# Two layers in a fast bilinear scheme: the first block's loads, casts and product order, and the order and additions of the last block

## The chip, the cores and the metric

The kernel runs on one core of a Trainium2 chip. A core has a matrix engine (TensorE, PE in the profile; its weight loads are the row PEld), VectorE (DVE), ScalarE (ACT), GpSimd (POOL) and SyncE (SP), which issues transfers only; ACT and POOL issue transfers as well, each on queues of its own. The metric is the device time of one execution in microseconds. Before the change the median of three runs is 852.05 us (851.43 to 852.44).

## The reference

```python
# x [16,512,768], w1 [768,3072], b1 [3072], w2 [3072,768], all float32, normal draws
y = np.matmul(x, w1) + b1
y = np.maximum(y, 0)
return np.matmul(y, w2).astype(np.float32)
```

The 16 x 512 rows of x are one matrix of 8192 rows. So two products of 8192 x 768 x 3072 and 8192 x 3072 x 768 are computed, with a bias and a ReLU between.

## The kernel before

**Scheme.** Both layers use a bilinear scheme with fewer products than the plain one: sums and differences of blocks of x and of w1 (and of y and of w2) are formed on VectorE, multiplied on TensorE in float16, and combined again by VectorE and ACT. Tables at the top of the file hold which sums are formed (`X_SUMS`, `W1_SUMS`, `Y_SUMS`, `W2_SUMS`), which products are taken, and in which order (`FIRST_ORDER`, `SECOND_ORDER`, and `LAST_ORDER` for the last block).

**Blocks.** There are 16 iterations: two halves (chunks) of the 3072 hidden columns, and in each the eight blocks of 1024 rows. An iteration computes the hidden layer of its block (per group of hidden columns, gi = 0 and 1, 20 products in place of 24, each of six matmuls of 128 x 256, L1071) and then eight outputs (26 products in place of 32, each of six matmuls of 128 x 384, L1197). Output number `to` is 256 rows by 384 columns. The sums of x are at L826, of w1 at L842, of w2 at L860, of y at L1044.

**First block (iteration 0).** Its first layer is computed plainly, since no sums exist yet (`first_block`, `add_plain`, products at L981). The prologue issues the loads: four tiles of 128 rows of x as float32 into the slots `s` (L711; tiles 0 and 2 on SP's queue, 1 and 3 on ACT's), the bias as 24 rows of 128 on ACT's queue behind them (L679), then on POOL's queue, which casts to float16 on the way, three strips of w1 of group 0 (each 768 rows by two lots of 128 columns in `v1`, L685), the lower 512 rows of x as float16 into `xn` (L706), the strips of group 1, and w2 (L691). x of the first block is turned on TensorE: three 128 x 128 transposes fill a bank (L923), VectorE copies one half of the columns of a tile to `x` (L931) and ACT the other (L929). The upper four tiles are turned in float32, the lower four in float16. `add_bias` turns the bias rows on TensorE (L943), copies them to `b1y` (L946), squares them (L949) and fills the tables of bias combinations (L957, L961), all of the latter on VectorE. In `first_block` it is added between the first and the second half of the first bank. Each bank takes 12 matmuls of 256 columns, six per 256 rows of x, and is then evicted by ACT with bias and ReLU into `y`. Later blocks get x turned by the DMA queue of SP (L758).

**Order.** A planner (`Graph`) receives the tasks with costs, and keys that they read and write. TensorE runs its tasks in the order in which they were added; the tasks of the other engines are put in order by a simulation with these costs, in which `presets` gives the times at which the first loads are taken to land (bias rows at 5.0, x tiles at 5.3 and 7.2, w1 strips from 9.3 on). The result is a fixed order of instructions for each engine with semaphores between them. PSUM has eight banks; `Reg` stands for one or two of them, or for one of nine slots of `s`.

**Second chunk and last block.** The outputs of the first chunk are stored plainly. Those of the second are added to them: by default by an accumulating transfer, issued by POOL (L1250; L1253 stores the part of an output apart from its last product). In the last iteration the operations in `LAST_DIRECT` go another way: `add_priors` reads the stored output back by SP into the space of x (L1172), `prior_task` adds the kept sum to it on VectorE (L1258), `operation` adds the product's bank (L1214), and SP stores the result plainly (L1248). The last output goes in two halves, stored on ACT's and on SP's queue (L1243). An operation that is also in `LAST_FOLD` has the stored output added into its bank on VectorE ahead of the chain's last product (`fold`), and is then copied out by ACT (L1208). Before the change `LAST_FOLD` names operations 6 and 7, neither of which is in `LAST_DIRECT`, so no fold takes place. `SECOND_OPS` gives the outputs: operation 5 makes output 1, operation 0 output 2, operation 1 output 3, operation 2 output 4, operations 6 and 7 outputs 6 and 7.

At the end a flag, computed from sums of squares of all inputs, decides whether a general path runs; with these inputs it doesn't.

Of the kernel before, what the change touches and what calls it, by code (L numbers as in the profile page):

```python
# [10 lines left out]
FP16 = mybir.dt.float16  # L11
# [3 lines left out]
ACTF = mybir.ActivationFunctionType  # L15
# [3 lines left out]
P = 128  # L19
# [567 lines left out]
class Fast:  # L587
# [93 lines left out]
    def load_strip(self, to, c, g, h):  # L681
# [26 lines left out]
    def prologue(self):  # L708
        nc = self.nc
        for s in range(4):  # L710
            (nc.sync, nc.scalar)[s % 2].dma_start(out=self.s[:, s],  # L711
                                                  in_=self.xf[s * P:(s + 1) * P, :])
        self.load_bias()
        self.load_strip(self.v1, 0, 0, 0)
        self.constants()
        self.load_strip(self.v1, 0, 0, 1)
        self.load_strip(self.v1, 0, 0, 2)
        self.load_x(0, 1, 2)
        for h in range(3):
            self.load_strip(self.v1, 0, 1, h)  # L720
        for q in range(4):
            for h in range(3):
                self.load_w2(self.v2, 0, h, q)
        self.load_x(1, 0)
        for _ in range(8):
            nc.tensor.matmul(self.ps[:, 7, 0:P], lhsT=self.ones, rhs=self.ones, start=True,
                             stop=True)

    def presets(self):
        g = self.g  # L730
        for t, at in enumerate((9.3, 11.3, 13.3, 19.9, 21.8, 23.8)):
            for k in range(2):
                g.preset(("w1", t // 3, 2 * (t % 3) + k), at)
# [171 lines left out]

    def add_transpose_first(self, half, s):

        for a in range(2):  # L910
            ps = Reg("ps", leaves=0)

            def view(ps=ps):
                p = self.ps[:, ps.at[0], :]
                if half:
                    p = p[:, 0:3 * P // 2].bitcast(FP16)
                return p[:, 0:3 * P].rearrange("p (k m) -> p k m", k=3)

            def turn(a=a, view=view):
                ident = (self.ident, self.ident16)[half]  # L920
                rows = self.xn[:, 4 + s, :] if half else self.s[:, s]
                for k in range(3):
                    self.nc.tensor.transpose(view()[:, k, :],  # L923
                                             rows[:, (3 * a + k) * P:(3 * a + k + 1) * P], ident)

            def copy(a=a, view=view):
                out = self.x_part(4 * half + s)[:, 3 * a:3 * a + 3]
                if a:
                    self.nc.scalar.copy(out=out, in_=view())  # L929
                else:  # L930
                    self.nc.vector.tensor_copy(out=out, in_=view())  # L931
            r = 2 * half + s // 2
            self.g.add("PE", 210 if half else 380, turn, writes=[ps],
                       reads=[("xn", 4 + s)] if half else [("rows", s), self.hold[s]])
            self.g.add("ACT" if a else "DVE", 560, copy, reads=[ps],
                       writes=[("x", 2 * r + a, s % 2)])

    def add_bias(self):
        nc = self.nc
# [29 lines left out]
    def add_plain(self, strip, j, m, parts, evict_parts, between=None):  # L969
        gi, h = divmod(strip, 3)  # L970
        ps = Reg("ps", leaves=2 if parts == 1 else 0)
        nc = self.nc
# [13 lines left out]
        def evict(a, b):  # L986
            n = 4 * h + 2 * gi + j
            i = 8 * m + 2 * gi + j
            out = self.y[:, i:i + 5:4, h * self.QM:(h + 1) * self.QM]
            nc.scalar.activation(out=out[:, a:b],  # L990
                                 in_=self.ps[:, ps.at[0], :].rearrange("p (a m) -> p a m",
                                                                       a=2)[:, a:b],
                                 func=ACTF.Relu, bias=self.b1y[:, n:n + 1])
        for n in range(parts):
            rows = (0, 1) if parts == 1 else (n,)
            nc = self.nc
            self.g.add("PE", 1300 // parts, lambda n=n: product(n),
                       reads=[("x", 4 * m + 2 * r + k2, q) for r in rows for k2 in range(2)
                              for q in range(2)] + [("w1", gi, 2 * h + k) for k in range(2)],
                       writes=[ps])  # L1000
            if n == 0 and between:
                between()
        for a, b in ((0, 2),) if evict_parts == 1 else ((0, 1), (1, 2)):
            self.g.add("ACT", 692 if evict_parts == 1 else 470, lambda a=a, b=b: evict(a, b),
                       reads=[ps, "b1y"],
                       writes=[("y", (2 * m + r) * 4 + 2 * gi + j, h) for r in range(a, b)])

    def first_block(self):
# [534 lines left out]
```

## Time and profile before

| what | value |
|---|---|
| median of three runs | 852.05 us |
| profiled execution, whole | 851.03 us |
| its span | 849.4 us |
| TensorE matmuls busy | 839.5 us, 99% |
| TensorE weight loads busy | 625.1 us, 74% |
| VectorE busy | 736.5 us, 87% |
| ACT busy | 568.5 us, 67% |
| POOL busy | 166.5 us, 20% |
| mean granted TensorE clock | 0.999 |
| moved by DMA | 128.93 MB in 170968 packets |

The profile is one execution, taken by the hardware profiler. Its span runs from the first to the last instruction on record, the execution's own time has some more around it. In the rows of the timeline, the first two numbers are the start in us from the span's start and the duration; then engine, line, operation, tiles (written <- read), shapes and the count of instructions in the stretch. In square brackets stands the idle time ahead of it and what ended it. ACTq and SPq are the issue of a transfer by that engine. A row of the view that tells who waits for whom has engine, tile and line of the waiting instruction, the one waited for, and then the sum in us, the count and the longest wait. A row of windows begins with the stretch and its length; then come, for PE, PEld, DVE, ACT, POOL and SP in this order, the busy time (and the count of instructions), the granted clock, the DMA share and the GB/s. A row of DMA queues has packets, MB and the time of its packets as a share of 16 engines; a row of landing times the count, the KB of one and the median us from issue to landing.

### The profile page before, as it was taken

Reading aid. Unit: us, or ns where it says so; the run is one execution under the profiler, and the core shown is the slowest. Engines: PE = TensorE matmul, PEld = TensorE weight load, DVE = VectorE, ACT = ScalarE, POOL = GpSimd, SP = SyncE. Lnnn points to the kernel's source line nnn. Section 1 sums busy time; section 2 is a strip of 40 time slices with the busy share of each in tenths; the row PEclk is TensorE's granted clock in tenths of the full one; section 3 lists DMA queues with packets and bytes.
Section 4 is the critical chain, followed back from the end, with each engine's and each line's share of the span. In section 5 each row is a group of like instructions: output and inputs, shape, how many; then the busy total and the mean of one; then the engine's idle time right before and its main releaser. Section 6 shows DMA issues by size and latency. Waiting matters only on the chain.

```text
span 849.4 us, 16770 instructions
## 1 busy us (share of the span) xinstructions
PE 839.5 (99%) x6381; PEld 625.1 (74%) x6381; DVE 736.5 (87%) x1229; ACT 568.5 (67%) x1203; POOL 166.5 (20%) x181
## 2 busy tenths in 40 slices
PE   8999999999999999999999999999999999999997
PEld 7558778587786867768687686877868677686874
DVE  5898988969889697988999989698896979979787
ACT  5866967678686784946859477766657666456462
POOL 5210011102111020110031503224041230502301
PEclk9999999999999999999999999999999999999999
DMA  9996597969789496593894968979789797975937
GB/s 212 202 180 175 82 230 108 198 140 160 198 109 203 117 154 164 96 249 123 232 177 82 193 109 148 160 110 176 124 130 147 122 164 113 154 126 75 167 85 178
DMA packets 170968, 128.93 MB, mean 152 GB/s; under 512 B 93805, under 2 KB 169349, under 8 KB 170885
## 3 DMA queue, kind: packets, MB, share of 16 engines
q0 software_dynamic: 57104, 69.61, 53.3%
q1 hardware_dynamic: 113312, 57.23, 28.4%
q8 instruction: 50, 0.82, 0.4%
q10 hardware_dynamic: 468, 1.00, 0.3%
q14 instruction: 34, 0.27, 0.1%
HBM read 73.15 MB, written 69.60 MB: 168 GB/s over the span
## 4 chain that ended last, share of the span: by engine, by line


## 5 line engine op out<-in xcount | busy, mean ns | idle before, releaser
L1197 PE MATMUL ps<-v,y 128*128 128x384 f16 x2496 | 408.5, 326 | 0.5 <-ACT s L1208 0.5
L1071 PE MATMUL ps<-x,v 128*128 128x256 f16 x3600 | 395.6, 273 | 0.0
L1071 PEld LDWEIGHTS <-v 128*128 128x128 f16 x3600 | 352.0, 98 | 42.5
L1197 PEld LDWEIGHTS <-y 128*128 128x128 f16 x2496 | 244.0, 98 | 160.9 <-issue 1.0
L1208 ACT ACTIVATE s<-ps 128x384 f32<-128x384 f32 (+1 forms) x244 | 153.8, 643 | 137.4 <-PE ps L1197 136.3
L1044 DVE TENSOR_TENSOR y<-y 128x768 f16<-128x768 f16 (+1 forms) x384 | 219.0, 618 | 2.5
L1114 DVE CUSTOM_DVE_ANT_0 y<-ps,s 128x512 f16<-128x512 f32 x240 | 155.7, 685 | 54.2 <-ACT s L1111 41.9
L1250 POOL DMA_DIRECT2D out_dram<-s x79 | 95.2, 1467 | 166.7 <-ACT s L1208 112.7
L1111 ACT ACTIVATE s<-ps,bt 128x256 f32<-128x256 f32 x180 | 75.1, 469 | 63.2 <-PE ps L1071 57.4
L826 DVE TENSOR_TENSOR x<-x 128x768 f16<-128x768 f16 (+1 forms) x210 | 113.8, 578 | 1.4
L706 POOL DMA_DIRECT2D xn<-in_x_dram x30 | 25.1, 838 | 258.4 <-ACT xn L766 153.8
L1111 ACT ACTIVATE y<-ps,bt 128x256 f16<-128x256 f32 x180 | 69.6, 486 | 7.7 <-PE ps L1071 7.7
L1214 DVE TENSOR_TENSOR s<-ps,s 128x768 f32<-128x768 f32 x74 | 70.5, 952 | 1.7 <-PE ps L1197 0.9
L1208 ACT ACTIVATE ps<-ps 128x384 f32<-128x384 f32 (+1 forms) x144 | 68.1, 512 | 5.0 <-PE ps L1197 3.2
L1214 DVE TENSOR_TENSOR s<-s,ps 128x768 f32<-128x768 f32 x60 | 57.0, 950 | 2.8 <-PE ps L1197 0.5
L766 ACT ACTIVATE xn<-xn 128x768 f16<-128x768 f16 x64 | 53.5, 837 | 1.2 <-DMA x<-xn 1.2
L1253 POOL DMA_DIRECT2D out_dram<-s x16 | 18.9, 1184 | 108.6 <-ACT s L1208 97.3
L1111 ACT ACTIVATE ps<-ps,bt 128x256 f32<-128x256 f32 x60 | 26.7, 445 | 19.2 <-PE ps L1071 18.2
L1107 ACT ACTIVATE ps<-ps 128x512 f32<-128x512 f32 x60 | 35.3, 588 | 3.6 <-DVE y L1114 3.5
L1122 DVE TENSOR_TENSOR s<-s,ps 128x512 f32<-128x512 f32 x30 | 20.6, 687 | 17.8 <-PE ps L1071 17.8
L981 PE MATMUL ps<-x,v 128*128 128x256 f16 (+1 forms) x216 | 32.0, 308 | 0.7 <-DVE x L931 0.7
L1117 DVE SCALAR_TENSOR_TENSOR s<-ps,bt,s 128x256 f32<-128x256 f32 x60 | 26.1, 476 | 4.4 <-PE ps L1071 4.4
(59 smaller groups left out, 302.6 us busy)
## 6 DMA issues: line engine op xcount, KB each, us to landing
out_dram<-s POOLq DMA_DIRECT2D x95, 384.0 KB, 7.6
out_dram<-s SPq DMA_DIRECT2D x69, 384.0 KB, 4.6
xn<-in_x_dram POOLq DMA_DIRECT2D x28, 768.0 KB, 9.2
v<-in_w_dram POOLq DMA_DIRECT2D x6, 384.0 KB, 10.6
v<-in_w_dram POOLq DMA_DIRECT2D x12, 192.0 KB, 9.0
w1d<-in_w_dram POOLq DMA_DIRECT2D x6, 384.0 KB, 6.8
w2d<-in_w_dram POOLq DMA_DIRECT2D x12, 192.0 KB, 5.4
v<-w1d SPq DMA_DIRECT2D x12, 192.0 KB, 4.2
```

The source lines that it names most:

```text
L766: self.nc.scalar.activation(out=self.xn[:, s, :], in_=self.xn[:, s, :], func=ACTF.Square, accum_out=self.stat[:, self.stat_at["x"] + i:][: ...
L826: self.nc.vector.tensor_tensor(out=self.two(x, out), in0=self.two(x, in0), in1=self.two(x, in1), op=ALU.add if sign > 0 else ALU.subtract)
L981: nc.tensor.matmul(self.ps[:, ps.at[0], cols], lhsT=self.v1[:, gi, 2 * h + k2, k, j * P:(j + 1) * P], rhs=rhs, start=(k2 == 0 and k == 0), ...
L1044: self.nc.vector.tensor_tensor(out=self.two(self.y, out), in0=self.two(self.y, in0), in1=self.two(self.y, in1), op=ALU.add if sign > 0 els ...
L1071: nc.tensor.matmul(self.ps[:, at, j * self.QM:(j + 1) * self.QM], lhsT=self.v1[:, gi, self.w1s[c][gi][FIRST_V[p]], k, j * P:(j + 1) * P], ...
L1107: nc.scalar.activation(out=out, in_=ps, scale=float(a), func=func if kind == "out" else ACTF.Copy)
L1111: nc.scalar.activation(out=out[:, j], in_=ps[:, j], func=func, scale=float(a), bias=beta(j))
L1114: nc.vector._custom_dve(TENSOR_ADD_SAT, out=out, in0=ps, in1=s, s0=F_MAX, s1=0.0)
L1197: nc.tensor.matmul(self.ps[:, bank[ch].at[j], 0:NH], lhsT=self.y[:, ys[SECOND_U[p]], m0:m0 + P], rhs=self.v2[:, slot[SECOND_V[p]], h, :], ...
L1208: nc.scalar.activation(out=out, in_=ps, func=ACTF.Copy, scale=float(a))
L1214: engine.tensor_tensor(out=out, in0=in0, in1=in1, op=ALU.add if a == b else ALU.subtract)
L1250: nc.gpsimd.dma_start(out=rows, in_=out, accum_op=ALU.add)
```

## The change

There are two parts.

**First block.** The three column strips of w1 of group 0 become six row pieces (`load_part`: 128 rows by three lots of 256 columns, 0.197 MB as written). The upper four tiles of x are cast from float32 to float16 into slots 16 to 19 of `y` (`add_casts`, one half of the columns on VectorE, one on ACT) and then turned in float16, six transposes to a bank in place of three. The bias is added first of all. The 72 matmuls of six banks (three strips, two column lots each) no longer run bank by bank: `first_rows` holds six banks at once and runs with the row piece k outermost, so that each piece of w1 is used by six products for one or two row halves n before the next is needed; the six evictions come after all of them. The transposes of tiles 2 and 3 stand behind the first six products, those of the lower tiles behind the steps (4, 1) and (5, 1). `presets` gets landing times for the pieces.

**Last block.** `LAST_DIRECT` takes in operation 7: output 7 is read back, added on the chip and stored plainly. `LAST_FOLD` becomes operation 5. The last thirteen products of `LAST_ORDER` stand in another order.

```diff
-LAST_ORDER = (13, 15, 4, 17, 10, 8, 12, 18, 3, 0, 1, 14, 2, 19, 23, 21, 11, 16, 25, 22, 7, 9, 6,
-    24, 5, 20)
-LAST_FOLD = (6, 7)
-LAST_DIRECT = (0, 1, 2, 3, 4, 5)
+LAST_ORDER = (13, 15, 4, 17, 10, 8, 12, 18, 3, 0, 1, 14, 2, 19, 21, 11, 25, 23, 7, 16, 5, 6, 22,
+    9, 24, 20)
+LAST_FOLD = (5,)
+LAST_DIRECT = (0, 1, 2, 3, 4, 5, 7)
...
+    def load_part(self, g, k):
+        w1r = self.w1.rearrange("(k p) (h c) -> p k h c", p=P, c=4 * P)
+        self.nc.gpsimd.dma_start(out=self.v1[:, g, k // 3:6:2, k % 3, :],
+                                 in_=w1r[:, k, 0:3, 2 * g * P:2 * (g + 1) * P])
...
         self.load_bias()
-        self.load_strip(self.v1, 0, 0, 0)
+        self.load_part(0, 0)
         self.constants()
-        self.load_strip(self.v1, 0, 0, 1)
-        self.load_strip(self.v1, 0, 0, 2)
+        for k in range(1, 6):
+            self.load_part(0, k)
         self.load_x(0, 1, 2)
...
-        for t, at in enumerate((9.3, 11.3, 13.3, 19.9, 21.8, 23.8)):
+        parts = (8.2, 9.2, 10.2, 11.2, 12.3, 13.4)
+        for k in range(6):
+            g.preset(("part", k), parts[k])
...
+    def add_casts(self):
+        for s in range(4):
+            for a in range(2):
+                cols = slice(3 * a * P, 3 * (a + 1) * P)
+                def cast(s=s, cols=cols, a=a):
+                    out, rows = self.y[:, 16 + s, cols], self.s[:, s, cols]
+                    if a:
+                        self.nc.scalar.copy(out=out, in_=rows)
+                    else:
+                        self.nc.vector.tensor_copy(out=out, in_=rows)
+                self.g.add("ACT" if a else "DVE", 560 if a else 500, cast,
+                           reads=[("rows", s), self.hold[s]], writes=[("cast", s, a)], due=0.0)
+
+    def add_transpose_first(self, half, rows):
+        for s in rows:
             ps = Reg("ps", leaves=0)
...
+            def turn(s=s, view=view):
+                tile = self.xn[:, 4 + s, :] if half else self.y[:, 16 + s, :]
+                for k in range(6):
+                    self.nc.tensor.transpose(view(k // 3)[:, k % 3, :],
+                                             tile[:, k * P:(k + 1) * P], self.ident16)
...
+    def first_rows(self):
+        nc = self.nc
+        banks = {(h, j): Reg("ps", leaves=0) for h in range(3) for j in range(2)}
+        def product(k, n, h, j):
+            nc.tensor.matmul(self.ps[:, banks[h, j].at[0], n * self.QM:(n + 1) * self.QM],
+                             lhsT=self.v1[:, 0, 2 * h + k // 3, k % 3, j * P:(j + 1) * P],
+                             rhs=self.x[:, 2 * n + k // 3, k % 3, :],
+                             start=(n == 0 and k == 0), stop=(k == 5), skip_group_check=True)
+        for k, n in ((0, 0), (1, 0), (0, 1), (1, 1), *((k, n) for k in range(2, 6) for n in range(2))):
+            for h, j in banks:
+                self.g.add("PE", 109, lambda k=k, n=n, h=h, j=j: product(k, n, h, j),
+                           reads=[("x", 2 * n + k // 3, q) for q in range(2)] + [("part", k)],
+                           writes=[banks[h, j]])
+            if (k, n) == (0, 0):
+                self.add_transpose_first(0, (2, 3))
+            elif (k, n) == (4, 1):
+                self.add_transpose_first(1, (0, 1))
+        self.add_transpose_first(1, (2, 3))
+        for h, j in banks:
+            self.add_evict(h, j, 0, banks[h, j], 1)
...
     def first_block(self):
-        for s in range(4):
-            self.add_transpose_first(0, s)
         plain = self.add_plain
-        for strip in range(3):
-            for j in range(2):
-                between = None
-                if strip == 0 and j == 0:
-                    between = self.add_bias
-                elif strip == 2 and j == 1:
-                    between = lambda: [self.add_transpose_first(1, s) for s in (0, 1)]
-                plain(strip, j, 0, 2, 2 if strip == 1 else 1, between)
-        plain(0, 0, 1, 2, 1, lambda: [self.add_transpose_first(1, s) for s in (2, 3)])
-        plain(0, 1, 1, 2, 1)
+        self.add_casts()
+        self.add_bias()
+        self.add_transpose_first(0, (0, 1))
+        self.first_rows()
+        for j in range(2):
+            plain(0, j, 1, 2, 1)
```

More of the change, by code (lines that the diff above doesn't have):

```diff
@@ L927, in copy @@
                 out = self.x_part(4 * half + s)[:, 3 * a:3 * a + 3]
                 if a:
-                    self.nc.scalar.copy(out=out, in_=view())
+                    self.nc.scalar.copy(out=out, in_=view(a))
                 else:
-                    self.nc.vector.tensor_copy(out=out, in_=view())
+                    self.nc.vector.tensor_copy(out=out, in_=view(a))
             r = 2 * half + s // 2
-            self.g.add("PE", 210 if half else 380, turn, writes=[ps],
-                       reads=[("xn", 4 + s)] if half else [("rows", s), self.hold[s]])
@@ L935, in add_transpose_first @@
-            self.g.add("ACT" if a else "DVE", 560, copy, reads=[ps],
-                       writes=[("x", 2 * r + a, s % 2)])
+            self.g.add("PE", 420, turn, writes=[ps],
+                       reads=[("xn", 4 + s)] if half else [("cast", s, a) for a in range(2)])
+            for a in range(2):
+                self.g.add("ACT" if a else "DVE", 480, lambda a=a, copy=copy: copy(a), reads=[ps],
+                           writes=[("x", 2 * r + a, s % 2)])
     def add_bias(self):
@@ L984, in product @@
                                      stop=(k2 == 1 and k == 2))
[L986 to L993, printed above, removed]
         for n in range(parts):
@@ L1002, in add_plain, with add_evict, evict @@
                 between()
+        self.add_evict(strip, j, m, ps, evict_parts)
+    def add_evict(self, strip, j, m, ps, evict_parts):
+        gi, h = divmod(strip, 3)
+        nc = self.nc
+        def evict(a, b):
+            n = 4 * h + 2 * gi + j
+            i = 8 * m + 2 * gi + j
+            out = self.y[:, i:i + 5:4, h * self.QM:(h + 1) * self.QM]
+            nc.scalar.activation(out=out[:, a:b],
+                                 in_=self.ps[:, ps.at[0], :].rearrange("p (a m) -> p a m",
+                                                                       a=2)[:, a:b],
+                                 func=ACTF.Relu, bias=self.b1y[:, n:n + 1])
         for a, b in ((0, 2),) if evict_parts == 1 else ((0, 1), (1, 2)):
```

23 lines of the change are left out of this document (8 added, 15 removed).

## The prediction

> **What bounds the kernel now.** I read the page first, then who waits for whom on TensorE, then the timeline of both ends.
>
> ```profile
> span 849.4 us, 16770 instructions
> ```
> ```profile
> PE ps L923 <- DMA s<-in_x_dram: 1.1, 2, 0.6
> PE ps L981 <- DVE x L931: 0.7, 2, 0.4
> PE ps L1197 <- ACT s L1208: 0.5, 1, 0.5
> ```
> Between its first product and its last, TensorE waits twice in all: 0.35 us for an x copy in the first block (the longer of the two L981 waits) and 0.5 us once for ACT. So everything in between is TensorE's own work, the change leaves that work as it is, and only two stretches can pay: the way to the first products, and what follows the last one. The change touches both. First the start, from the timeline:
>
> ```profile
> 1.51 0.99 POOL L685 DMA_DIRECT2D v<-in_w_dram  x1 [0.83 <-POOLq L1527]
> 1.87 0.65 ACTq L679 DMA_DIRECT2D b_rows<-in_b_dram  x1
> ...
> 6.96 2.50 POOL L685 DMA_DIRECT2D v<-in_w_dram  x3
> ...
> 7.68 1.50 PE L923 MATMUL ps<-ident,s 128*128 128x128 f32 x12 [0.52 <-DMA s<-in_x_dram]
> 8.23 1.21 DVE L931 CAST x<-ps 128x384 f16<-128x384 f32 x2 [0.81 <-PE ps L923]
> ...
> 9.50 0.82 PE L981 MATMUL ps<-x,v 128*128 128x256 f16 x6 [0.32 <-DVE x L931]
> ...
> 10.24 0.24 PE L943 MATMUL ps<-ident,b_rows 24*128 24x24 f32 x1
> ...
> 10.41 6.72 PE L981 MATMUL ps<-x,v 128*128 128x256 f16 x60
> 10.52 0.18 DVE L946 COPY b1y<-ps 128x24 f32<-128x24 f32 x1 [1.07 <-PE ps L943]
> ...
> 12.15 0.18 DVE L949 TENSOR_TENSOR stat<-b1y 128x24 f32<-128x24 f32 x1
> ...
> 16.97 0.83 PE L923 MATMUL ps<-ident,xn 128*128 128x128 f16 x12
> ...
> 17.49 0.61 DVE L931 COPY x<-ps 128x384 f16<-128x384 f16 x2
> 17.51 0.86 ACT L929 COPY x<-ps 128x384 f16<-128x384 f16 x2 [0.30 <-PE ps L923]
> ...
> 17.64 1.59 PE L981 MATMUL ps<-x,v 128*128 128x256 f16 x12
> ...
> 20.26 12.11 PE L981 MATMUL ps<-x,v 128*128 128x256 f16 x88 [0.35 <-DVE x L931]
> ```
> The first product starts at 9.50, when x is copied and the first strip of w1 has landed. The bias is turned only at 10.24, between products, and waits for nothing. The 20.26 row starts the second half of the first bank over the lower x rows; by then 78 products and 24 float16 transposes are done. I measure the new start against this point, because behind it TensorE's order is the same.
>
> **The start, step by step.** The order of instructions that the change builds has one thing that the diff does not show at a glance: the bias transpose is TensorE's first instruction behind the warm-up, ahead of all x transposes, since the bias is now added first. It waits for the bias rows, and TensorE runs in order. When do these land? Their issue has no landing of its own in the trace, but their queue shows it: they are the last issue of ACT's queue (q10), behind two x tiles. The DMA view of 7.0 to 7.2 us, then that of 7.2 to 7.6, then landing times (the rows begin with the issues of 1.44 on SP and 1.51 on POOL):
>
> ```profile
> q0 software_dynamic: 73, 0.04, 136.7%
> q10 hardware_dynamic: 6, 0.00, 4.6%
> q1 hardware_dynamic: 3, 0.00, 2.1%
> ```
> ```profile
> q0 software_dynamic: 156, 0.08, 146.2%
> ```
> ```profile
> s<-in_x_dram SPq DMA_DIRECT2D x1, 384.0 KB, 6.1
> v<-in_w_dram POOLq DMA_DIRECT2D x1, 384.0 KB, 7.8
> ```
> q10 moves its last six packets, the tail of the bias, between 7.0 and 7.2. SP's queue (q1) has its last packets in the same 0.2 us, and its second x tile, the last thing on it, counts as landed at 1.44 + 6.1 = 7.54. So the bias lands at about 7.55 (bounds 7.2, the last packet, and 7.8), not at the 5.0 that the planner's table assumes. Then:
>
> - TensorE starts the bias transpose 0.1 later, as it did at 7.68 behind the x tile of 7.54: 7.66. It takes 0.17 (10.24 to 10.41). Twelve float16 transposes follow, 7.83 to 8.6: a group of twelve holds TensorE for 0.7 (16.97 to the next product at 17.64).
> - The casts of rows 0 and 1 (VectorE and ACT, from 5.5) are done long before and cost nothing; TensorE's wait covers them. But VectorE's next instructions are the bias copy and four table entries, ahead of the x copies. The copy starts 0.28 behind the transpose (10.24, 10.52): 7.94. All 13 bias operations took 10.52 to 12.33, 1.81; the first five take 0.7: 8.64. The two x copies from float16 banks take 0.61: 9.3. First product 0.06 later, as at 9.50 behind 9.44: **9.4**.
> - The first w1 piece is no limit. Strip 0 landed at 1.51 + 7.8 = 9.3 and the queue moves a piece per us:
> ```profile
> 8.00:9.00 1.00, 1.00 (x11) 0.94 (x9) 0.67 (x2) 0.44 (x1) 1.00 (x2) 1.00 1.44 194
> ```
>  194 GB/s as written, so a piece of 0.197 MB takes 1.0: piece 0 at 8.3, piece k at 8.3 + k. From 9.4 on every piece is there when TensorE comes to it, and so the finer loading, worth 1.2 (9.5 to 8.3) by itself, buys nothing.
> - Six products (0.65; sixty took 10.41 to 16.87), twelve transposes (0.7), six products (0.65): 11.4. The next six read the copies of rows 2 and 3. VectorE does, behind 9.3, two casts, eight bias operations (1.13), two copies (0.61). A float32 to float16 cast inside SBUF is in no row; the nearest are the same width from PSUM:
> ```profile
> L685 POOL DMA_DIRECT2D v<-in_w_dram x4 | 3.3, 866 | 0.0
> ...
> L931 DVE CAST x<-ps 128x384 f16<-128x384 f32 x4 | 2.2, 557 | 6.0 <-PE ps L923 5.8
> ...
> L931 DVE COPY x<-ps 128x384 f16<-128x384 f16 x4 | 1.3, 352 | 0.3 <-PE ps L923 0.3
> ```
>  0.35 to 0.56 each; I take 0.45, between them, as the source is float32 but not PSUM. Copies done at 9.3 + 0.9 + 1.13 + 0.61 = 11.94, next product 12.0: a new wait of 0.6 (0.4 to 0.8).
> - Then 60 products (6.46), two groups of transposes (1.4), six products (0.65): 20.5. The wait of 0.35 before the 20.26 product shrinks, as six products now stand behind the transposes, but ACT has two evictions ahead of its copies: 0 to 0.4, I take 0.2. That product starts at 20.7.
>
> The start is **0.5 slower** (bounds: 0.4 faster with every value at its low end, 1.2 slower with all at the high end), where with the bias out of the way it would gain.
>
> POOL's queue: six issues stand in place of three ahead of x's lower rows, so the strips of group 1, issued from 6.96 on, go out up to 2.6 later (three issues of 0.87). That is covered twice: at the rate above the DMA queue still has pieces to 13.3 and x's lower half (0.79 MB, 4 us) to 17.3 in front of them; and behind the 20.26 row TensorE has 66 products of group 0 left, 7 us, before it reads one. Without the cover it would be 2.6 us of TensorE. The six products of a step now hold six of the eight PSUM banks to the last piece, so six evictions come at once; the 0 to 0.4 above is what they cost.
>
> [...]
>
> **The end, step by step.** VectorE in the last stage, and the stores (timeline, windows of 3 and 5 us, the DMA view of the first of them, landing times):
>
> ```profile
> 817.58 25.51 PE L1197 MATMUL ps<-v,y 128*128 128x384 f16 x156
> ...
> 828.51 0.95 DVE L1214 TENSOR_TENSOR s<-s,ps 128x768 f32<-128x768 f32 x1
> 829.38 1.96 DVE L1044 TENSOR_TENSOR y<-y 128x768 f16<-128x768 f16 x4
> ...
> 837.42 1.19 POOL L1250 DMA_DIRECT2D out_dram<-s  x1 [5.63 <-DVE s L1214]
> ...
> 841.24 2.81 DVE L1214 TENSOR_TENSOR s<-ps,x 128x768 f32<-128x768 f32 x4
> ...
> 844.11 0.34 SPq L1243 DMA_DIRECT2D out_dram<-s  x1
> ```
> ```profile
> 839.50:842.50 3.00, 3.00 (x21) 1.81 (x19) 2.91 (x4) 0.00 (x0) 0.00 (x0) 1.00 1.08 131
> 842.50:847.50 5.00, 0.59 (x4) 0.14 (x2) 1.54 (x3) 0.00 (x0) 0.00 (x0) 1.00 1.06 388
> ```
> ```profile
> q0 software_dynamic: 245, 0.37, 104.3%
> ```
> ```profile
> out_dram<-s SPq DMA_DIRECT2D x1, 384.0 KB, 2.5
> ...
> out_dram<-s SPq DMA_DIRECT2D x1, 192.0 KB, 4.2
> ```
> Output 7's accumulating store (837.42) has the engines to itself from 839.5 to 842.5, at 131 GB/s and a share of 1.08: it blocks the plain stores. These then run packed at 388 GB/s until 847.5, so the last half store, issued at 844.11, lands 4.2 later, 848.3, and the span ends 1.1 after that. Added on the chip, output 7 is a plain store six products earlier, and this jam is gone.
>
> The price is VectorE's: behind operation 17 (828.51) it has one prior addition, output 7's sum and the fold more, and output 1's sum less: two operations net, while TensorE's waits in this stretch no longer hold it. It is behind TensorE all the way: from 829.38 four y sums (0.47 each by the x4 row), fourteen float32 operations (0.9; the four at 841.24 start 0.92 and 0.87 apart) and two halves (1.0): 844.9 on TensorE's old clock, or 844.5 at 0.87 each. I take 844.7, against 844.05 now. By the same count the fold ends at 839.4; the product that it must precede, the 24th of 26 (0.98 each, the last ending at 843.1), starts at 840.15: 0.75 to spare, and TensorE pays only for what is late beyond that. Output 1's sum goes to ACT instead, which has nothing else to do there.
>
> Then the store of output 2 goes out at 843.75 and, with the engines free, lands 2.5 later (the store of 837.42), with two half stores of 0.5 each behind it: 847.25, and with the 1.1 the span ends at 848.35: **1.1 saved** (0.3 if VectorE is 0.4 later and the stores queue 0.4, 1.6 if the halves overlap). SP gains one prior load, among those ahead of the last products, and one store; POOL loses two.
>
> **Sum.** 849.45 + 0.5 - 1.1 = 848.85 of span. The profiled execution took 851.03 in all, 1.6 more than its span and 1.0 below the median of 852.05. Taken off the median: 852.05 - 0.6 = **851.5**. Under 0.2% (1.7 us) this kernel's runs, 1.0 apart, don't tell from no change. Its own range, by the bounds of both ends and the runs' spread, is 850.3 to 852.8.
>
> **The rivals.**
> - The bias lands early, by 6 us, as the planner's table has it. Then piece 0 decides: first product at 8.4, next wait about nil, 1.0 earlier than my 9.4 and 0.5 less waiting: the start gains 1.0, the sum 2.1: 849.95. Against it: q10's packets up to 7.2. Chance 0.13.
> - Slower: VectorE's casts of rows 2 and 3 (9.3 to 10.2) are held by POOL, which then issues the strips of group 1. Up to one issue (0.87) in front of each cast, 1.7 in all, straight into the wait before the products of rows 2 and 3: 852.05 + 0.5 + 1.7 - 1.1 = 853.15. It decides from 0.6 of delay on. For it: both stand at the same time; against it: the issues are not gapless there. [...] Chance 0.12.
> - The jam goes but another takes its place: six stores in 8 us still queue, and the span ends 5.4 behind VectorE as now: 852.05 + 0.5 + 0.65 = 853.2. Against it: 1 us of transfer each, over a us apart. Chance 0.1.
>
> **How the numbers follow.** My forecast 0.62, the rivals as given, 0.03 for others. Faster by over 0.2% (below 850.35) takes most of the first rival and a tenth of the forecast: 0.20. Slower (above 853.75) has parts of the second and third and the forecast's upper end: 0.11. The rest, 0.69, is within. Range 849.7 to 853.5, from the first rival to the others, and 0.3 beyond each, since the runs are 1.0 apart.
>
> **What would show it.** Right: TensorE's bias transpose waits for the bias DMA until past 7.4; first product after 9.2; a wait for VectorE near 12; the product of 20.26 later than before; TensorE's last product 0.5 later; no accumulating store after 832; the last half store lands under 3.2 after its issue. Wrong: a bias transpose before 6, or a VectorE end over 1.9 behind TensorE's.

## The result and the profile after

The changed kernel takes 852.7 us (median of 20 runs, 851.83 to 853.73) against 851.02 for the kernel before (20 runs, 850.42 to 852.84): the ratio is 1.0018, 95% interval 1.0011 to 1.0024. It is 1.7 us slower; the forecast was 0.6 faster. The profiled execution took 852.76, with a span 1.8 longer. The executions of one kernel can fall into groups: in the first run below they lie 1.9 us apart (850.28 to 850.75 with a mean granted clock of 0.999 to 1.0, 851.93 to 852.55 with 0.996 to 0.998); so profiles are compared by their rows below, and medians with that in mind.

First the span of after, and who waits for whom on TensorE there (engine, tile and line of the waiting one; sum, count, longest):

```profile
span 851.2 us, 16770 instructions
```
```profile
PE ps L966 <- DMA b_rows<-in_b_dram: 2.8, 1, 2.8
...
PE ps L1043 <- ACT x L951: 1.2, 1, 1.2
PE ps L1004 <- DVE x L953: 0.3, 1, 0.3
```

The bias transpose waits for its DMA, as forecast; the first product waits for ACT and not for VectorE; the wait near 12 isn't there. Now the start in the timeline of after:

```profile
7.88 0.21 PE L966 MATMUL ps<-ident,b_rows 24*128 24x24 f32 x1 [2.81 <-DMA b_rows<-in_b_dram]
...
8.02 0.85 PE L945 MATMUL ps<-ident,y 128*128 128x128 f16 x12
...
8.78 0.61 DVE L953 COPY x<-ps 128x384 f16<-128x384 f16 x2
9.15 2.56 POOL L685 DMA_DIRECT2D v<-in_w_dram  x3
9.16 0.86 ACT L951 COPY x<-ps 128x384 f16<-128x384 f16 x2 [2.77 <-DVE x L953]
9.31 0.92 DVE L929 CAST y<-s 128x384 f16<-128x384 f32 x2
...
10.07 1.44 PE L1043 MATMUL ps<-x,v 128*128 128x256 f16 x6 [1.20 <-ACT x L951]
...
11.31 1.49 PE L945 MATMUL ps<-ident,y 128*128 128x128 f16 x12
...
12.59 7.51 PE L1043 MATMUL ps<-x,v 128*128 128x256 f16 x54
...
19.94 0.83 PE L945 MATMUL ps<-ident,xn 128*128 128x128 f16 x12
...
23.71 11.66 PE L1004 MATMUL ps<-x,v 128*128 128x256 f16 x84 [0.30 <-DVE x L953]
```

Two things show. ACT's x copies begin at 9.16, when VectorE's copy of the same bank ends (8.78 and the 0.35 that one copy takes: 9.13), though the bank was full by 8.87, where the transposes end. And TensorE is slow: six products hold it from 10.07 to 11.31, 1.24 where six took 0.65 before; twelve transposes from 11.31 to 12.59, 1.28 for 0.7; 54 products from 12.59 to 19.94, 7.35, where 60 had taken 6.56 (10.41 to 16.97). The windows of 1 us say why (the last three columns are granted clock, DMA share and GB/s):

```profile
8.00:9.00 1.00, 0.87 (x13) 0.73 (x13) 0.81 (x6) 0.00 (x0) 1.00 (x2) 0.86 1.36 166
9.00:10.00 1.00, 0.00 (x0) 0.00 (x0) 1.00 (x4) 0.84 (x3) 1.00 (x2) 0.50 1.44 194
...
14.00:15.00 1.00, 1.00 (x7) 0.67 (x6) 0.93 (x3) 0.97 (x2) 0.49 (x1) 0.50 1.17 209
15.00:16.00 1.00, 1.00 (x8) 0.77 (x7) 1.00 (x3) 0.41 (x2) 0.34 (x1) 0.72 1.15 209
16.00:17.00 1.00, 1.00 (x12) 0.89 (x10) 0.84 (x2) 0.00 (x0) 0.37 (x1) 1.00 1.21 197
```

The granted clock is 0.50 from before 9 until past 15. By the shares of the two part windows it fell at 8.72 (0.86 in the window from 8) and was back at 15.56 (0.72 in that from 15), 6.8 later. So it fell at the end of the first transposes, ahead of the second gap, which begins at 8.87. In before it read 1.00 in all these rows; the one from 14, with eleven matmuls where after has seven:

```profile
14.00:15.00 1.00, 1.00 (x11) 0.89 (x10) 0.97 (x2) 1.00 (x4) 0.32 (x1) 1.00 1.19 212
```

The product that started at 20.26 now starts at 23.71, 3.45 later (forecast: 0.44).

The end, from the timeline, the windows of 3 us and the landing times of the last 9 us of after:

```profile
821.72 24.53 PE L1243 MATMUL ps<-v,y 128*128 128x384 f16 x149
...
845.57 1.88 DVE L1260 TENSOR_TENSOR s<-ps,x 128x768 f32<-128x768 f32 x3
...
847.48 0.34 SPq L1289 DMA_DIRECT2D out_dram<-s  x1
```
```profile
839.00:842.00 3.00, 3.00 (x21) 1.80 (x19) 3.00 (x4) 0.86 (x2) 0.00 (x0) 1.00 0.39 137
842.00:845.00 3.00, 3.00 (x20) 1.76 (x19) 3.00 (x5) 1.53 (x2) 0.00 (x0) 1.00 0.69 248
```
```profile
out_dram<-s SPq DMA_DIRECT2D x1, 192.0 KB, 2.6
```

TensorE ends at 846.25 (821.72 + 24.53), 3.15 later than the 843.10 of before; VectorE 1.2 behind it (845.57 + 1.88 = 847.45); the DMA engines are no longer full in these six us, and the last half store lands 2.6 behind its issue instead of 4.2. From TensorE's end to the span's end are 4.95 instead of 6.3. So 3.15 lost ahead of TensorE's end and 1.35 gained behind it make the 1.8.

### The profile page after: what moved, and what is told of

The parts are those of the page before. It is cut to its first block, busy times and chain, and to the rows that moved or that the text cites. A ratio compares the mean times of both kernels' runs of the same rounds, so it can differ in the third digit from the quotient of the medians.

```text
span 851.2 us, 16770 instructions
## 1 busy us (share of the span) xinstructions
PE 840.5 (99%) x6381; PEld 625.8 (74%) x6381; DVE 738.5 (87%) x1235; ACT 569.5 (67%) x1205; POOL 166.5 (20%) x182
## 5 line engine op out<-in xcount | busy, mean ns | idle before, releaser
L1296 POOL DMA_DIRECT2D out_dram<-s x78 | 93.9, 1476 | 164.8 <-ACT s L1254 108.7
L776 ACT ACTIVATE xn<-xn 128x768 f16<-128x768 f16 x64 | 53.5, 837 | 0.4 <-DMA x<-xn 0.4
L1299 POOL DMA_DIRECT2D out_dram<-s x15 | 17.9, 1192 | 107.2 <-ACT s L1254 98.3
L1153 ACT ACTIVATE y<-ps 128x512 f16<-128x512 f32 x30 | 17.9, 596 | 16.7 <-PE ps L1117 16.6
```

Of the source, the lines that this page charges most:

```text
L776: self.nc.scalar.activation(out=self.xn[:, s, :], in_=self.xn[:, s, :], func=ACTF.Square, accum_out=self.stat[:, self.stat_at["x"] + i:][: ...
L1153: nc.scalar.activation(out=out, in_=ps, scale=float(a), func=func if kind == "out" else ACTF.Copy)
L1296: nc.gpsimd.dma_start(out=rows, in_=out, accum_op=ALU.add)
```

## The experiments

The question was whether the lost start is the clock (theory A) or the order of the work (theory B), and whether the end gains by itself. Each median stands with its ratio to the kernel before, run beside it (850.78 to 850.94).

**TensorE kept busy until the bias lands.**
```diff
-        for _ in range(8):
+        for _ in range(13):
             nc.tensor.matmul(self.ps[:, 7, 0:P], lhsT=self.ones, rhs=self.ones, start=True,
```


> The changed kernel with 13 in place of 8 warm-up matmuls, nothing else. They fill TensorE's idle stretch from 5.07 to 7.88 but for 0.4 us. Theory A (the lost time is the granted clock: it read 0.50 from 9 to 15 us, and 31 matmuls ran at twice their spacing, 0.213 for 0.109 and 0.107 for 0.056): the clock stays at 1.00, the first product still starts near 10.1, the product that started at 23.71 starts near 21.1, and the time is 852.7 - 2.6 = 850.1. Theory B (the lost time is the order: products start late and wait for x copies and pieces whatever the clock): the product of 23.71 stays within 0.5 and the time stays at 852.2 to 853.

Measured: 851.93 (1.0005, 0.9996 to 1.0014). Five of its eleven executions took 850.28 to 850.75, six 851.93 to 852.55. The profiled one, of 850.28, in the timeline:

```profile
7.88 0.21 PE L966 MATMUL ps<-ident,b_rows 24*128 24x24 f32 x1 [0.67 <-DMA b_rows<-in_b_dram]
8.02 0.84 PE L945 MATMUL ps<-ident,y 128*128 128x128 f16 x12
10.11 0.81 PE L1043 MATMUL ps<-x,v 128*128 128x256 f16 x6 [1.25 <-ACT x L951]
10.76 0.83 PE L945 MATMUL ps<-ident,y 128*128 128x128 f16 x12
11.43 6.08 PE L1043 MATMUL ps<-x,v 128*128 128x256 f16 x54
...
21.12 5.15 PE L1004 MATMUL ps<-x,v 128*128 128x256 f16 x42 [0.31 <-DVE x L953]
```

The order is that of the changed kernel and the first product starts as late, but the six products take 0.65, the transposes 0.67, the 54 products to 17.34 5.91: 0.59, 0.61 and 1.44 less, 2.64 together, and the later product starts at 21.12, 2.59 earlier. In this execution theory A has its number (850.28 for 850.1), and theory B falls. The median didn't come, since six of the eleven are some 1.9 slower. The mean granted clock on record for each execution parts the two groups: 0.999 to 1.0 in the five, 0.996 to 0.998 in the six. That the six lose it in the gaps of 0.67 and 1.25 is tested in the sixth run.

**The bias moved back behind the first x transposes.**
```diff
         self.add_casts()
-        self.add_bias()
         self.add_transpose_first(0, (0, 1))
+        self.add_bias()
...
-        g.preset("b1_rows", 5.0)
+        g.preset("b1_rows", 7.9)
```


> The changed kernel with the bias transpose behind the x transposes of tiles 0 and 1, and the planner told that the bias rows land at 7.9. Both the idle stretch and the wait for the bias ahead of x go. Theory A: the clock stays at 1.00; the x transposes start near 6.4, the first product at 8.4 when piece 0 has landed, 1.7 earlier than 10.07; with the 2.65 of clock the product of 23.71 starts near 19.5 and the time is 852.7 - 4.2 = 848.5. Theory B: only the 1.7 of the earlier first product comes back: 851.0. If the clock still falls (TensorE idles from 7.1 to 8.4), 850 or more.

Measured: 850.83 (0.9999, 0.999 to 1.0008). The first product starts at 8.47, the x transposes at 6.02, as expected of both; but TensorE is now idle 0.97 and 1.02 around the transposes, and the clock falls all the same, at 8.32 by the 0.66 of the window from 8: the windows of 9 to 11 read 0.50, and six products take 1.25 (8.47 to 9.72). The product behind the lower rows starts at 21.03, hardly earlier than 21.12 above. So the time is near theory B's 851.0, but it came the third way that was expected, with a clock that still falls. Against the first run the first product is 1.64 earlier, and the half pace takes 1.55 of that back: 0.60 on the six products, 0.61 on the transposes, 0.34 on the 54 products (11.00 to 17.25).

**Each part alone.** The kernel before with the three tables `LAST_ORDER`, `LAST_FOLD` and `LAST_DIRECT` of the change, and the changed kernel with those of before.

> The kernel before with the last block's part of the change alone. Theory A and my account of the end agree: VectorE ends 0.4 later, the span ends 1.6 earlier behind it, so 1.2 below the kernel before, 849.8. Rival (the end gains nothing by itself, what looks like a gain comes from the shifted start): 851.0.

> The changed kernel with the last block's three tables as before. Theory A and my account of the start: 3.0 above the kernel before, 854.0, with the clock at 0.50 from about 9 to 15 us. Rival (the two parts are not additive): 852.7, as the changed kernel.

Measured: the end alone 849.67 (0.9985, 0.9976 to 0.9994), 1.27 faster, with the last half store landing 2.6 behind its issue; the start alone 854.46 (1.0037, 1.0024 to 1.0051), 3.5 slower. So the end's gain is no echo of the shifted start. In the start alone products run at half pace (six from 10.67 to 11.90, 1.23 in place of 0.65), though the clock column reads 1.00 in the windows from 10 and from 11. The sum of the parts, 2.25, is 0.6 above the 1.7 of the whole, within the spread of the five executions of the start alone (853.46 to 854.72). The end alone is the fastest kernel of this study: it beats both.

The profiled execution of the end alone, of 851.08, is one of the four that took 850.62 to 851.35, where the other seven took 848.85 to 849.71. Its start is that of the kernel before, and the timeline shows what such an execution loses:

```profile
6.18 4.55 PE L923 MATMUL ps<-ident,s 128*128 128x128 f32 x24 [1.11 <-DMA s<-in_x_dram]
```

The gap ahead of the transposes is 1.11 in place of 0.59, the 24 take 4.55 in place of 2 x 1.50, most of them at half pace (the windows of 1 us from 7, 8 and 9 have 7 matmuls each, where that from 8 had 11 before), and the product of 20.26 starts at 21.80. So the start of before, too, ran at half pace in this execution; the clock's column reads 1.00 there.

**All put together.** The second run's order, the bias tables added only behind the x copies of tiles 2 and 3, and matmuls that fill gaps:
```diff
+    def keep(self, count):
+        ps = Reg("ps", leaves=0)
+        def busy():
+            for _ in range(count):
+                self.nc.tensor.matmul(self.ps[:, ps.at[0], 0:P], lhsT=self.ones, rhs=self.ones,
+                                      start=True, stop=True)
+        self.g.add("PE", 220 * count, busy, writes=[ps])
...
-        for _ in range(8):
+        for _ in range(10):
...
         self.add_transpose_first(0, (0, 1))
+        self.keep(4)
         self.add_bias()
+        self.keep(1)
         self.first_rows()
```


> The changed kernel with the bias behind the x transposes of tiles 0 and 1 (as in the second run), the bias tables behind the x copies of tiles 2 and 3, and extra matmuls that fill the gaps: 10 warm-up matmuls, 4 ahead of the bias transpose, 1 behind it. Theory A: spacing stays at 0.109 from the first product on, which starts near 8.5; against the run with 13 warm-ups, whose first product starts at 10.11 and whose undisturbed executions took 850.3 to 850.75, that is 1.5 less: 848.9, some 2 below the kernel before, and the executions no longer fall into two groups. Theory B (only order counts): 850.8, as the run with the bias moved back.

Measured: 850.25 (0.9991, 0.9983 to 1.0), and all eleven between 850.01 and 850.75: one group. That is 1.35 above theory A's 848.9 and 0.55 below theory B's 850.8. The start is what A expects, but the gain is mostly given back later; TensorE's waits and its timeline:

```profile
PE ps L1261 <- ACT s L1272: 1.0, 1, 1.0
```
```profile
8.52 0.83 PE L1058 MATMUL ps<-x,v 128*128 128x256 f16 x6
...
9.86 6.06 PE L1058 MATMUL ps<-x,v 128*128 128x256 f16 x54
16.59 0.84 PE L945 MATMUL ps<-ident,xn 128*128 128x128 f16 x12 [0.68 <-DMA xn<-in_x_dram]
...
19.25 6.99 PE L1019 MATMUL ps<-x,v 128*128 128x256 f16 x59
```

Six products of 0.65 behind 19.25 bring the row to 19.90, 1.2 ahead of the 21.12 of the first run, yet the span of 848.5 is only 0.2 shorter than that run's 848.7. TensorE is now ahead of the load of x's lower rows, and it waits 1.0 for ACT at 155 us, in the second block. There ACT stands with a square of x (L776) behind a DMA transpose of x (1.76 in the sixth run's timeline, which has the same wait), while a drain that TensorE needs is queued behind it.

**Gaps filled without a change of order**, in the changed kernel (15 warm-up matmuls, 6 between the transposes and the first product) and in the kernel before (9 warm-ups, 3 and 2 behind the pairs of x transposes).

> The changed kernel, its order untouched, with 15 warm-up matmuls and 6 more between the x transposes of tiles 0 and 1 and the first product: both idle stretches, 2.81 and 1.20, are filled. Theory A: with 13 warm-ups five of eleven executions took 850.3 to 850.75 and six 851.9 to 852.6, since a gap of 0.7 and one of 1.25 were left; with these filled all fall into the lower group: median 850.5. If the gaps don't matter for the groups, the median stays near 851.9.

> The kernel before with its three gaps filled in the same way (9 warm-up matmuls, 3 behind the transposes of tiles 0 and 1, 2 behind those of tiles 2 and 3). Theory A: TensorE's waits between its first product and its last stay as they are and the clock is held already in most executions; the median stays at 850.9, and the executions of 851.6 to 852.6 (seven of 27) go. If the matmuls put in delay x, 0.2 to 0.6 more.

Measured: the changed kernel so filled takes 851.7 (1.0006, 0.9998 to 1.0015), its executions 850.94 to 852.07: the gap between two groups is gone, no execution has a mean clock under 0.998, and the products run at full pace (54 from 11.54 to 17.58). But the level is 1.2 above the lower group of the first run, not equal to it, and so near the 851.9 that was expected if the gaps didn't matter; the clocks and the pace tell the two apart, the median doesn't. Its profile has the wait of 1.0 for ACT at 156 us, which the first run's doesn't have, and its later product starts 0.23 later: 1.2 of span. The kernel before so filled takes 852.14 (1.0015, 1.0006 to 1.0024), more than I had allowed: its product of 20.26 comes 0.35 later, and the wait of 0.5 for ACT has grown to 1.0, together 0.9 of the 1.1 by which its span is longer. So here filling only cost, 1.25 by the medians, and the mean clock on record is much the same: 0.996 to 1.0, for 0.997 to 0.999 in the kernel before.

**One edit of the change in the kernel before: the bias first.**
```diff
+        self.add_bias()
         for s in range(4):
             self.add_transpose_first(0, s)
...
-                    between = self.add_bias
+                    between = None
```


> The kernel before with one thing of the change alone: the bias is added first, ahead of all x transposes (the float32 transposes, strips, product order and end stay). Theory A: TensorE idles from 5.07 to 7.88, the clock falls; the 24 float32 transposes, 0.11 apart now, run in part at 0.21, the first product starts near 12 or later, and the time is 851 + 2.5 to 4.5. Theory B (in-order wait alone): transposes 7.95 to 10.7, first product 11.2 in place of 9.5, 852.7.

Measured: 854.73 (1.0039, 1.0026 to 1.0052), 3.8 slower, within A's range and 2 above B's. The float32 transposes, 24 in 2 x 1.50 before, in the timeline, and one of the windows of 1 us over them:

```profile
8.31 0.27 PE L943 MATMUL ps<-ident,b_rows 24*128 24x24 f32 x1 [3.24 <-DMA b_rows<-in_b_dram]
8.52 5.38 PE L923 MATMUL ps<-ident,s 128*128 128x128 f32 x24
13.91 7.40 PE L981 MATMUL ps<-x,v 128*128 128x256 f16 x66
```
```profile
10.00:11.00 1.00, 1.00 (x7) 1.00 (x6) 0.80 (x5) 0.65 (x2) 0.70 (x1) 1.00 1.45 196
```

5.38 for 24: half pace throughout, and the first product at 13.91 in place of 9.50. Half pace alone isn't the mark of this edit, since the third run's profile shows it too; but all five executions, 853.87 to 855.48, lie above theory B's 852.7. So putting the bias first makes a loss of this size by itself, without casts, pieces or held banks. The window's clock column reads 1.00 all the while; here the pace of the instructions, 0.224 each for 0.125, is the better witness.

**The plan, the loads and the banks.**

> As the fifth run (bias and tables moved back, gaps filled), but the planner counts the filling matmuls as taking no time. In the fifth run TensorE's products came 1.2 earlier than in the run with 13 warm-ups and the span was only 0.2 shorter, since TensorE then waited 0.98 at 155 us for ACT, which stood behind a DMA. If that wait comes from the planner's order: it goes, and the time is 849.3. If it hangs on when that DMA lands: it stays, and the time is 850.2.

> As the ninth run, and the first half of x's lower rows is loaded ahead of the last piece of w1. In the fifth run TensorE waited 0.68 at 15.9 for those rows, which landed at 16.54. Expected: they land near 14.6, the last piece near 15.5, the wait goes, and the time is 0.6 below the ninth run. If the last piece then comes too late for its products at about 16.5, the gain is nil.

> The run with 13 warm-ups, with a PSUM bank of its own for each half of tiles 0 and 1, as before the change. There ACT's x copies waited for VectorE's copies out of the same bank (ACT 9.16, VectorE done 9.14), and the first product for ACT until 10.11. If sharing the bank is what orders them: ACT copies from about 8.5, the first product starts near 9.4, 0.7 earlier, and the lower group of times falls from 850.4 to 849.8. If the copies wait for something else, the first product stays at 10.1.

The ninth is the fifth with `keep` added at a cost of 0. It takes 850.78 (0.9998, 0.9989 to 1.0007) and still waits 0.9 at 155.7 us, for which 850.2 was expected: the planner's view of the filling isn't what makes that wait. The tenth loads in another order:
```diff
-        for k in range(1, 6):
+        for k in range(1, 5):
             self.load_part(0, k)
-        self.load_x(0, 1, 2)
+        self.load_x_part(0)
+        self.load_part(0, 5)
+        self.load_x_part(1)
```
It takes 852.94 (1.0024, 1.0014 to 1.0035), a miss that its timeline explains:

```profile
15.68 0.83 PE L951 MATMUL ps<-ident,xn 128*128 128x128 f16 x12
...
16.67 3.27 DVE L858 TENSOR_TENSOR v<-v 128x768 f16<-128x768 f16 x6 [4.75 <-DMA v<-in_w_dram]
...
19.86 0.61 DVE L959 COPY x<-ps 128x384 f16<-128x384 f16 x2
20.27 0.83 PE L951 MATMUL ps<-ident,xn 128*128 128x128 f16 x12 [2.18 <-DVE x L959]
```

The rows came early enough (transposes at 15.68), but on VectorE six sums of w1 stood ahead of the x copies and waited for the last piece until 16.67; the copy came at 19.86, and TensorE lost 2.18. The eleventh gives each half of tiles 0 and 1 a bank (`Reg`) of its own, in the first run's kernel. It takes 851.12 (1.0004, 0.9995 to 1.0013); the profiled execution, in the timeline:

```profile
8.55 0.69 DVE L955 COPY x<-ps 128x384 f16<-128x384 f16 x2
8.72 0.86 ACT L953 COPY x<-ps 128x384 f16<-128x384 f16 x2 [2.18 <-PE ps L947]
...
9.30 0.82 PE L1047 MATMUL ps<-x,v 128*128 128x256 f16 x6 [0.28 <-DVE x L955]
...
10.29 0.71 DVE L984 TENSOR_SCALAR bt<-b1y 128x8 f32<-128x8 f32 x3
...
12.51 1.25 PE L1047 MATMUL ps<-x,v 128*128 128x256 f16 x10 [1.05 <-DVE x L955]
```

ACT now waits for TensorE alone, and the first product starts at 9.30: sharing the bank was what ordered the copies. Of the 0.8 some 0.2 isn't the bank's: the planner now also puts VectorE's copies ahead of the table entries, at 8.55 in place of 8.78. The lower group of times, 850.45 to 850.8, didn't fall to the 849.8 that was expected. The gain is lost again at 12.51, twelve products further, where the next x copies stand behind the bias tables on VectorE.

**The end without output 7 on the chip.** The end alone, with operation 7 out of `LAST_DIRECT`.

> The third run's kernel (the last block's part alone), but operation 7 is taken out of those added on the chip: output 7 goes back to accumulating stores from POOL, the new product order and the fold of operation 5 stay. VectorE has one addition of 0.87 less behind operation 17. If the accumulating store's hold on the DMA engines was what cost the end (my account): it comes back between the plain stores, the last half store lands 1 us or more later behind its issue than the 2.6 of the third run, and the time is 850.3 to 850.9. If the new order and the fold alone made the gain: the same 2.6, and 849.0 to 849.7.

Measured: 850.01 (0.9989, 0.998 to 0.9998), below the range of my account. Its profiled execution has the start of before (first product at 9.49), and a span of 848.0, 1.4 shorter. The accumulating store in the timeline, the windows, and the last landing:

```profile
835.30 1.19 POOL L1250 DMA_DIRECT2D out_dram<-s  x1 [3.77 <-ACT s L1208]
```
```profile
836.00:839.00 3.00, 3.00 (x20) 1.80 (x19) 3.00 (x5) 0.61 (x2) 0.48 (x1) 1.00 0.71 79
839.00:842.00 3.00, 3.00 (x20) 1.75 (x18) 1.73 (x3) 1.61 (x2) 0.00 (x0) 1.00 1.05 318
```
```profile
out_dram<-s SPq DMA_DIRECT2D x1, 192.0 KB, 2.9
```

The store is there, but issued at 835.30 instead of 837.42, and the engines are back to plain stores (318 GB/s) in 839 to 842, where before 839.5 to 842.5 moved 131 GB/s. The last half lands 2.9 behind its issue, 0.3 more than the 2.6 of the third run and not 1. From TensorE's end (843.00) to the span's end are 5.0, as in the changed kernel. So most of the end's gain is the new order with the fold, which moves the accumulating store out of the way; whether adding output 7 on the chip is worth the remaining 0.3 between 850.01 and 849.67 these runs can't tell.

## Why the prediction was wrong

The step that failed is in "The start, step by step": "a group of twelve holds TensorE for 0.7", "Six products (0.65; sixty took 10.41 to 16.87)", "60 products (6.46)". All these durations came from rows with the granted clock at 1.00 (windows from 9 to 18 of before), and were used behind an idle stretch of TensorE that the same text had worked out. I priced the wait for the bias as a delay of the first product, and left out that float32 transposes at 5.66 and 7.68 were also what kept TensorE busy between the warm-up and the first product. With them gone it is idle from 5.07 to 7.88, the clock falls at 8.72, and TensorE is idle again from 8.87 to 10.07; its work from there to 15.56 runs at half pace. The price is 2.64 by the first run's rows.

The other steps in turn:
- **The bias lands late and stands first**: right. 7.88 for 7.66; it is the edit from which the loss comes (eighth run).
- **First product at 9.4**: 10.07. VectorE's part was right (x copies done at 9.39 for 9.3). Not seen was that two tiles' halves in one bank put ACT's copies behind VectorE's, some 0.6 of the 0.8 that the eleventh run gained.
- **The pieces are no limit**: right; no product waited for one in the changed kernel.
- **A new wait of 0.6 near 12**: it didn't show, and not in the first run at full pace either: there the first product was 0.7 later than forecast, so that the copies were in time. With clock and banks mended it is there, 1.05 at 12.51 (eleventh run).
- **The wait before the product of 20.26**: 0.2 forecast, 0.30 measured.
- **What is in between stays as it is**: not quite. The 0.49 for ACT at 155 us is gone in the changed kernel, and ran from nil to 1.05 in the others.
- **The end saves 1.1**: right in size (1.27 by itself; 1.35 by the profile, with VectorE 1.2 behind TensorE, where 843.10 to 844.05 had been 0.95). Its cause as I gave it, output 7's store gone, was too narrow: the new order with the fold does most of it. TensorE's last product came 3.15 later in place of 0.5, and with it POOL's last store (833.60, where none was to be after 832).
- **Two small slips that change no step**: the bias operations from 10.52 to 12.33 are 14 and not 13, and sixty products take 6.56, since 16.87 is where a weight load starts.
- **Rivals**: the bias early: no. Another jam at the end: no. VectorE's casts held by POOL: no run shows the 1.7 or what would hold a cast, which was my assumption; what shows is one cast 0.3 longer than the other. The two casts took 0.92, 0.46 each for my 0.45, so the sum was right; but the second took 0.65 of it. Here it stands in the timeline of after, with the issue of POOL beside it, and then the same two casts in the eleventh run:

```profile
9.15 0.92 POOL L685 DMA_DIRECT2D v<-in_w_dram  x1
...
9.58 0.65 DVE L929 CAST y<-s 128x384 f16<-128x384 f32 x1
```
```profile
9.17 0.62 DVE L929 CAST y<-s 128x384 f16<-128x384 f32 x2
```

The second cast ends at 10.23, 0.16 behind POOL's issue (10.07); in the eleventh run both take 0.62 together, from 9.17 to 9.79, though POOL issues from 9.20 on there.

The forecast of 851.5 stood on the 852.05 of three runs. Off the 851.02 of the 20 runs it is 850.4, so the measured time is 2.3 above the forecast and not 1.2: that it lies well inside the range is in part luck.

With the clock held and all else as in the change, the lower group of the first run is 850.28 to 850.75, 0.4 below the median before, for a forecast of 0.6: the forecast without its missing term. That it comes so near is luck in part: the product of 20.26 starts 0.86 later there for my 0.44, and against that stand an end that gains 1.35 for my 1.1 and a wait of 0.49 for ACT that is gone.

What is left open: what decides whether the DMA transpose at 155 us lands in time for ACT. It isn't the time at which TensorE gets there nor the planner's cost of the filling, and no run tells more. Nor do these runs say at which gap the clock falls: it fell behind 2.81, and in the second run's profile behind 0.97 and 1.02, but not in the first run's behind 0.67 and 1.25.

## To carry to other kernels

Here an idle stretch of 2.81 ahead of a dense one cost TensorE 2.64 more behind its end, by the half pace. So count what the removed instructions did for the clock, not only their time, and hold every duration of a row against the clock that it was taken at. Before an instruction is put first on an engine, look up when its input lands: twelve x transposes, whose casts were done by 6.39, stood behind the bias until 8.02. Ahead of late data, have work that is ready stand in front. And a gain at the start must be followed through each queue behind it: the second, ninth and eleventh run gained 0.8 to 1.7 at the first product and lost nearly all of it within the first block or at 155 us.

## What the runs showed of the hardware

- In the changed kernel's profile the clock fell 0.84 behind the end of a gap of 2.81 (7.88 to 8.72) and read 0.50 for 6.8 us, to 15.56. In the second run's, with gaps of 0.97 and 1.02, it fell at 8.32 and was back at 11.72, by the 0.66 and 0.64 of the windows from 8 and from 11: 3.4 us. In the first run's, with gaps of 0.67 and 1.25, it read 1.00 in every window from 5 to 26; the mean clock on record of that kernel is 0.999 or 1.0 in five executions and 0.996 to 0.998 in the other six. With one gap of 0.59 ahead of the first product (sixth run) it is 0.998 to 1.0 in all eleven. What sets the lengths of 3.4 and 6.8, and why executions of one kernel differ, no run shows.
- The granted clock's column read 1.00 where 24 float32 transposes ran at half pace (eighth run, 5.38 in place of 2 x 1.50). The 16 warm-up matmuls, float32 of the same shape, took 3.78 in the kernel before and in the changed one, about the same pace, with the column at 1.00 too. So the column showed the half pace of the changed kernel, at 0.50, and not that of these rows; why, no run shows.
- In the changed kernel's profile two of VectorE's four casts took 0.36 and 0.35 (from 5.47 and 9.31). The other two took 0.60 and 0.65 and ended at 6.34 and 10.23, 0.17 and 0.16 behind the end of an issue of POOL (6.17 and 10.07). In the eleventh run two casts took 0.62 together while POOL issued. So an issue of POOL beside a cast isn't enough to make it longer.
- With an accumulating store of 384 KB issued 2.1 us earlier, in the new order (twelfth run), the last plain store landed 2.9 behind its issue in place of 4.2.
